# A two-layer hybrid encoder on one core: the mixers' modulation pieces stand earlier in the weight order

## The chip, the cores and the metric

One core of a Trainium2 chip runs the whole program. The metric is device time in microseconds (us) of one execution, as the median of several runs. Engines are named as the profile names them: PE is TensorE's matmul, PEld its weight load, DVE is VectorE, ACT is ScalarE, POOL is GpSimd, SP is SyncE, which here only issues DMAs.

## The reference

The kernel computes two layers on one sequence of 256 tokens with 1024 channels, all in float32. Cut to what matters here:

```
mod = silu(c) @ ada_w + ada_b                       # c is one row; ada_w is 1024 x 6144 per layer
sh_m, sc_m, gt_m, sh_f, sc_f, gt_f = split(mod, 6)
h = rms_norm(x, g_pre_mix) * (1 + sc_m) + sh_m
rq, rk, rv, rg, lx, ly, fq, fk, fv, ff, gates = split(h @ w_in)
y_ret = silu(rg) * head_norm(retention(rope(rq), rope(rk), rv))
y_lru = gelu(ly) * rg_lru(causal_conv(lx))
y_fox = forgetting_attention(fq, fk, fv, log_sigmoid(ff + b_f))
merged = g0 * (y_ret @ ret_w_o) + g1 * (y_lru @ lru_w_o) + g2 * (y_fox @ fox_w_o)     # g = sigmoid(gates)
x = x + gt_m * rms_norm(merged @ w_out, g_post_mix)
h = rms_norm(x, g_pre_mlp) * (1 + sc_f) + sh_f
x = x + gt_f * rms_norm(square(relu(h @ w1)) @ w2, g_post_mlp)
```

The first half of a layer is called the mixer, the second the MLP. `mod` is a product of one row with a large matrix: its weights must be read (24 MB per layer), but there is little to compute. `gt_m`, `sc_f` and `sh_f` are first used at the end of the mixer.

## The kernel before

**Weights come in pieces.** Every weight matrix is cut into pieces of 1 MB. A piece is loaded as two halves of 512 KB (128 partitions x 1024 float32, tile `wraw`) by the DMA queue of SP. There are five `wraw` buffers (`NRAW`). All pieces of the program stand in one list, `ORDER`, and both the loads and the preparation of the pieces follow it.

**What happens to a matmul piece** (an entry `gemm`). Each half is split in a high and a low part, because three matmuls of rounded operands replace one in float32: ACT casts it to the high part (L241) and DVE subtracts that from the original (L242); both write one of four `wpair` buffers (`NHL`). The subtraction is the last reader of the `wraw` buffer, so it frees it for the next load. PE then runs the three products of each pair (L364, L365, L366), 48 matmuls of 256 columns for a piece. A result lies in PSUM (`ps`, two buffers for most pieces, four of another pool for `lx`, `ly` and the attention) until DVE or ACT has taken it out.

**What happens to a modulation piece** (an entry `ada`). PE has no part in it. DVE multiplies each half with the row of `silu(c)` and sums along it in one instruction (L296), which also frees the buffer; a small addition of the bias follows (L292). A part such as `gt_m` is four pieces. ACT does nothing for it.

**What sets the order.** Each engine runs its own instructions in the order that the program's scheduler has written down; an instruction that waits holds up all behind it on its engine. Pieces are asked for one or two ahead of their matmuls: `prefetch` walks `ORDER`, splits what is a matmul piece and sums what is a modulation piece as it comes to it. `weight_order` builds the list: within a mixer, `spread` puts the modulation pieces evenly between the matmul pieces from position `n - MIXR[l][0]` to position `n - MIXR[l][1]`, with n = 53 matmul pieces in the mixer of layer 0 and 61 in that of layer 1. The MLPs have their own modulation pieces (`MLPR`).

**The mixer's order of matmul pieces** after the first ones is `rg0..3 g12 w_r0..3 g13 ly0..3 fq0 w_l0..3 fv0..3 fq1..3 fk0..3 g20..3 w_f0..3 w_o0..3` (with `lru` before `rg`). During `rg`, `g12` and `w_r` DVE also runs the gates of the recurrent branch (L710 to L715) and its scan (L723 to L728); during `ly` the gelu (L903 to L906, and L678 for the low part of its result, `yll`). `w_l0` needs the results of all four `ly`. From `fk1` on the heads of the forgetting attention run beside the weights (L950 to L991).

Layer 0 has 12 modulation pieces in its mixer (`gt_m`, `sc_f`, `sh_f`, 24 halves), layer 1 has 8 (`sc_f`, `sh_f`, 16 halves). Before, they stand from behind `fv1` to ahead of `g23` in layer 0, and from behind `fv3` to ahead of `g23` in layer 1.

Of the kernel before, what the change touches and what calls it, by code (L numbers as in the profile page):

```python
# [69 lines left out]
def mix_order(l):  # L70
    first = 'g0 g0 g0 g0 lx lx g1 lx g1 lx lru' if l == 0 else \
            'rv rv rv rv rq rk g0 rq rk g0 lx g0 lx g0 lx g1 lx lru g1'
    rest = 'rg rg rg rg g1 w_r w_r w_r w_r g1 ly ly ly ly fq w_l w_l w_l w_l fv fv fv fv fq fq fq fk fk fk fk ' \
           'g2 g2 g2 g2 w_f w_f w_f w_f w_o w_o w_o w_o'
    order = first.split() + rest.split()
    return [(n, order[:i].count(n)) for i, n in enumerate(order)]
# [10 lines left out]
    return name in ('rv', 'w_o', 'w2') or (name == 'w1' and cix < 4)  # L87


MIXR = ((22, 8), (20, 8))  # L90
MLPR = ((5, 28), (5, 15))


def weight_order():
    order = [(n, 0, k) for k in range(KD) for n in ('ada_row', 'row')]

    def spread(l, gem, ada, lo, hi):
        at = [lo + (hi - lo) * i // max(len(ada), 1) for i in range(len(ada))]
        for i, (n, c) in enumerate(gem):
            order.append(('gemm', l, n, c))  # L100
            while at and at[0] <= i:
                at.pop(0)
                order.append(ada.pop(0))
        assert not ada

    for l in range(L):
        n = len(mix_order(l))
        parts = [(l, p) for p in ('gt_m', 'sc_f', 'sh_f')][l:]
        spread(l, mix_order(l), [('ada',) + p + (c,) for p in parts for c in range(4)], *(n - i for i in MIXR[l]))
        parts = [(l, 'gt_f')] + [(i, p) for i in range(l + 1, L) for p in ('sc_m', 'sh_m', 'gt_m')]  # L110
# [1109 lines left out]
```

## Time and profile before

| what | us |
|---|---|
| median of 3 runs (1123.99 to 1126.6) | 1125.44 |
| the profiled execution's own time | 1126.98 |
| its span, first to last instruction | 1125.2 |
| PE busy in the span | 1096.8 (97%) |
| DVE busy | 870.1 (77%) |
| ACT busy | 617.5 (55%) |
| DVE's 82 sums of modulation halves (L296 on `wraw`), busy | 100.0 |
| DVE idle ahead of them, until a DMA landed | 44.6 |

Times in the profile count from the first instruction. Layer 0's mixer lies between about 60 and 375 us, layer 1's between about 580 and 925 us. A matmul row lasts 0.28 us, but the next one starts 0.11 us after it, so PE's pace is read from starts, and a busy share of 5.00 in 5 us says only that no gap was longer than a matmul. An idle time in brackets behind a row says how long the engine stood before it and who ended that.

### The profile page before, as it was taken

What the parts mean: (1) busy time and instruction counts of PE and PEld (TensorE: products, weight loads), DVE (VectorE), ACT (ScalarE), POOL (GpSimd) and SP (SyncE); (2) the same over time, 40 slices, a digit from 0 to 9 for tenths busy, and PEclk for the clock granted to TensorE, in tenths of its full rate; (3) what the DMA queues carried; (4) which work ended last, traced back from release to release, by engine and by line L of the source; (5) the groups of instructions that cost most, each with busy time, mean ns of one, the idle gap of its engine ahead of it and who ended that gap; (6) DMA issues with size and microseconds to landing.
All of it is one profiled execution on the core that took longest, in us unless ns stands there. A gap on an engine that the chain in (4) does not pass through costs nothing.

```text
span 1125.2 us, 20478 instructions
## 1 busy us (share of the span) xinstructions
PE 1096.8 (97%) x8164; PEld 1034.8 (92%) x8164; DVE 870.1 (77%) x1324; ACT 617.5 (55%) x924; POOL 43.7 (4%) x60
## 2 busy tenths in 40 slices
PE   6999999999999999999999999999999999999997
PEld 5999999998899889989879999999999997989986
DVE  6998788878887789888586768887868788866543
ACT  6676695544455645444455658755434655645441
POOL 0001000000000210000030010000000002000000
PEclk9999999999999999999999999999999999999999
DMA  9954646679876569998845465566777584875641
GB/s 359 408 179 155 197 136 216 193 248 314 282 249 220 193 214 323 332 327 295 299 140 185 151 194 162 185 207 194 235 248 265 193 290 133 283 269 197 195 159 59
DMA packets 74284, 255.43 MB, mean 227 GB/s; under 512 B 10108, under 2 KB 12492, under 8 KB 74188
## 3 DMA queue, kind: packets, MB, share of 16 engines
q1 hardware_dynamic: 74188, 254.12, 67.2%
q8 instruction: 64, 1.05, 0.4%
q14 instruction: 32, 0.26, 0.1%
HBM read 253.00 MB, written 1.09 MB: 226 GB/s over the span
## 4 chain that ended last, share of the span: by engine, by line
PE 75%; DVE 9%; DMA 8%; issue 4%; ACT 3%; POOL 1%; DVEq 0%; POOLq 0%; SPq 0%; ACTq 0%
PE ps L366 22%; PE ps L365 22%; PE ps L364 22%; DMA wraw<-in_wts_dram 7%; DVE wpair L242 3%; DVE wraw L296 1%; ACT wpair L241 1%; ACT junk L445 1%; PE rvp L364 1%; PE rvp L365 1%; PE rvp L366 1%; POOL rs_v L199 1%; PE qkp L365 1%; PE qkp L364 1%; PE qkp L366 1%
## 5 line engine op out<-in xcount | busy, mean ns | idle before, releaser
L242 DVE TENSOR_TENSOR wpair<-wraw,wpair 128x1024 fp32r<-128x1024 f32 (+1 forms) x286 | 347.3, 1220 | 74.1 <-ACT wpair L241 72.7
L241 ACT CAST wpair<-wraw 128x1024 fp32r<-128x1024 f32 (+1 forms) x286 | 298.3, 1049 | 191.4 <-PE ps L366 122.5
L364 PE MATMUL ps<-hh,wpair 128*128 128x256 f32 x1312 | 364.9, 278 | 5.3 <-DVE fvl L678 2.8
L366 PE MATMUL ps<-hh,wpair 128*128 128x256 f32 x1312 | 363.4, 277 | 0.1
L365 PE MATMUL ps<-hl,wpair 128*128 128x256 f32 x1312 | 363.1, 277 | 0.0
L364 PEld LDWEIGHTS ps<-hh,wpair 128*128 128x128 f32 x1312 | 246.8, 188 | 6.5 <-DVE fvl L678 3.2
L366 PEld LDWEIGHTS ps<-hh,wpair 128*128 128x128 f32 x1312 | 246.5, 188 | 0.4 <-DVE wpair L242 0.3
L365 PEld LDWEIGHTS ps<-hl,wpair 128*128 128x128 f32 x1312 | 246.6, 188 | 0.2
L296 DVE SCALAR_TENSOR_TENSOR wraw<-wraw,sir 128x1024 f32<-128x1024 f32 x82 | 100.0, 1222 | 44.9 <-DMA wraw<-in_wts_dram 44.6
L241 ACT CAST wown<-wraw 128x1024 fp32r<-128x1024 f32 x72 | 74.7, 1048 | 62.4 <-DMA wraw<-in_wts_dram 40.6
L242 DVE TENSOR_TENSOR wown<-wraw,wown 128x1024 fp32r<-128x1024 f32 x72 | 87.4, 1222 | 26.2 <-ACT wown L241 25.9
L364 PE MATMUL ps<-wpair,mih 128*128 128x512 f32 x144 | 56.3, 391 | 0.0
L365 PE MATMUL ps<-wpair,mih 128*128 128x512 f32 x144 | 56.1, 389 | 0.0
L366 PE MATMUL ps<-wpair,mil 128*128 128x512 f32 x144 | 56.0, 389 | 0.0
L364 PE MATMUL ps<-wpair,hh 128*128 128x256 f32 (+1 forms) x144 | 45.6, 317 | 0.0
L365 PE MATMUL ps<-wpair,hh 128*128 128x256 f32 (+1 forms) x144 | 45.4, 316 | 0.0
L366 PE MATMUL ps<-wpair,hl 128*128 128x256 f32 (+1 forms) x144 | 45.4, 315 | 0.0
L364 PE MATMUL ps<-hh,wown 128*128 128x256 f32 x160 | 44.2, 276 | 0.0
L366 PE MATMUL ps<-hh,wown 128*128 128x256 f32 x160 | 44.2, 276 | 0.0
L365 PE MATMUL ps<-hl,wown 128*128 128x256 f32 x160 | 44.2, 276 | 0.0
L364 PE MATMUL ps<-wown,mih 128*128 128x512 f32 x112 | 43.7, 390 | 0.0
L365 PE MATMUL ps<-wown,mih 128*128 128x512 f32 x112 | 43.6, 389 | 0.0
(340 smaller groups left out, 2295.1 us busy)
## 6 DMA issues: line engine op xcount, KB each, us to landing
wraw<-in_wts_dram SPq DMA_DIRECT2D x440, 512.0 KB, 4.4
wfirst<-in_wts_dram SPq DMA_DIRECT2D x28, 512.0 KB, 10.2
rows<-drow SPq DMA_DIRECT2D x10, 512.0 KB, 5.0
xs<-in_x_dram SPq DMA_DIRECT2D x2, 512.0 KB
out_dram<-xs SPq DMA_DIRECT2D x4, 256.0 KB, 2.0
csb<-in_con_dram SPq DMA_DIRECT2D x1, 768.0 KB
csb<-in_con_dram SPq DMA_DIRECT2D x1, 256.0 KB, 10.1
vsb<-in_vec_dram SPq DMA_DIRECT2D x1, 152.0 KB
```

Source lines behind the costliest of these rows:

```text
L199: pin(nc.gpsimd.tensor_scalar(v, part, rest, None, ALU.add))
L241: A.copy(hi, t)
L242: V.tensor_tensor(lo, t, hi.bitcast(F32), ALU.subtract)
L296: V.scalar_tensor_tensor(t, t, 0.5, sir, ALU.mult, ALU.mult, accum_out=m)
L364: T.matmul(ps, ah, bh, start=start, stop=False, **kw)
L365: T.matmul(ps, ah, bl, start=False, stop=False, **kw)
L366: T.matmul(ps, al, bh, start=False, stop=stop, **kw)
L445: return A.activation(j, x, AF.Square, scale=D ** -0.5, accum_out=acc)
```

## The change

The two pairs of positions are other numbers; nothing else differs.

```
-MIXR = ((22, 8), (20, 8))
+MIXR = ((36, 14), (32, 14))
```

In layer 0 the 12 modulation pieces now stand from behind `w_r1` to behind `fk0`: `gt_m` among `w_r2..ly2`, `sc_f` among `fq0..w_l3`, `sh_f` among `fv0..fk0`; one comes to every 1.83 matmul pieces, before to every 1.17. In layer 1 the 8 pieces stand from behind `ly0` to behind `fq3`: one to 2.25 pieces, before one to 1.5. The number of loads, sums and matmuls is the same, and PE's instructions stand in the same order as before. The orders of DVE, SP and ACT change.

The first place is DVE's order in layer 0, from the end of `rg3` to the first half of `w_r1`'s weights (`wpair_1992`); `wraw_2057` and `wraw_2060` are the first modulation piece, `wraw_2129` is half of the second.

```order
+L296 SCALAR_TENSOR_TENSOR wraw_2057,mcol_2056<-wraw_2057,sir_84 128x1024
 L710 SCALAR_TENSOR_TENSOR lru_u_650<-ti_1902,lru_u_650 128x512
+L296 SCALAR_TENSOR_TENSOR wraw_2060,mcol_2056<-wraw_2060,sir_84 128x1024
 L712 SCALAR_TENSOR_TENSOR lru_a_652<-lru_a_652,lru_t_651 128x512
+L292 TENSOR_TENSOR mod0_111<-mcol_2056,vsb_83 128x2
 L714 TENSOR_SCALAR lru_a_652<-lru_a_652 128x512
 L715 TENSOR_SCALAR lru_t_651<-lru_t_651 128x512
 L710 SCALAR_TENSOR_TENSOR lru_u_650<-ti_1929,lru_u_650 128x512
 L712 SCALAR_TENSOR_TENSOR lru_a_652<-lru_a_652,lru_t_651 128x512
-L714 TENSOR_SCALAR lru_a_652<-lru_a_652 128x512
+L296 SCALAR_TENSOR_TENSOR wraw_2129,mcol_2128<-wraw_2129,sir_84 128x1024
 L242 TENSOR_TENSOR wpair_1992<-wraw_1990,wpair_1992 128x4x256
```

Three sums now stand ahead of the low part of `w_r1`, and the third reads a load that takes the place of the second.

The second place is DVE's order in layer 0 where the scan ends and the first half of `ly0`'s weights is split (`wpair_2274`); `wraw_2265` and `wraw_2268` are the third modulation piece. These are rows of the changed kernel.

```order
L296 SCALAR_TENSOR_TENSOR wraw_2265,mcol_2264<-wraw_2265,sir_84 128x1024
L725 TENSOR_TENSOR lru_u_650<-lru_u_650,lru_t_651 128x512
L872 SCALAR_TENSOR_TENSOR gate_699<-gate_699,ps_2214 128x512
L728 SCALAR_TENSOR_TENSOR lru_u_650<-lru_a_652,lru_u_650 128x256
L296 SCALAR_TENSOR_TENSOR wraw_2268,mcol_2264<-wraw_2268,sir_84 128x1024
L242 TENSOR_TENSOR wpair_2274<-wraw_2272,wpair_2274 128x4x256
```

Before, the split of this half stood ahead of these three scan and merge rows, and no sum stood near it.

The third place is DVE's order in layer 1, at the start of `ly`, in the changed kernel: `wpair_8470` and `wpair_8475` are the two halves of `ly1`, `wpair_8537` is the first half of `ly2`, and `wraw_8603` and `wraw_8606` are the second modulation piece.

```order
L242 TENSOR_TENSOR wpair_8470<-wraw_8468,wpair_8470 128x4x256
L296 SCALAR_TENSOR_TENSOR wraw_8603,mcol_8602<-wraw_8603,sir_84 128x1024
L296 SCALAR_TENSOR_TENSOR wraw_8606,mcol_8602<-wraw_8606,sir_84 128x1024
L242 TENSOR_TENSOR wpair_8475<-wraw_8473,wpair_8475 128x4x256
L242 TENSOR_TENSOR wpair_8537<-wraw_8535,wpair_8537 128x4x256
L292 TENSOR_TENSOR mod1_112<-mcol_8602,vsb_83 128x2
L903 SCALAR_TENSOR_TENSOR ge_8527<-ge_8527,ps_8478 128x512
```

Before, the splits of `ly1` and `ly2` followed one another here; now two sums of a piece that is loaded behind `ly2` stand between the halves of `ly1`.

## Rows read from the trace of the kernel before

**Rows 1.** Page, part 1: busy us, share of the span, instructions.
```profile
PE 1096.8 (97%) x8164; PEld 1034.8 (92%) x8164; DVE 870.1 (77%) x1324; ACT 617.5 (55%) x924; POOL 43.7 (4%) x60
```

**Rows 2.** Busy time by stretch: length, then PE, PEld, DVE, ACT, POOL; granted clock, DMA share, GB/s.
```profile
157.00:190.00 33.00, 32.87 (x290) 32.67 (x288) 29.90 (x42) 22.51 (x30) 0.00 (x0) 1.00 0.53 174
190.00:216.00 26.00, 26.00 (x232) 26.00 (x231) 20.95 (x26) 16.96 (x23) 0.00 (x0) 1.00 0.63 202
235.00:320.00 85.00, 79.64 (x666) 78.46 (x665) 72.19 (x148) 35.05 (x54) 0.00 (x0) 0.98 0.85 292
310.00:315.00 5.00, 5.00 (x32) 5.00 (x31) 4.52 (x8) 1.07 (x3) 0.00 (x0) 0.66 0.83 253
728.00:744.00 16.00, 16.00 (x144) 16.00 (x142) 14.70 (x20) 7.73 (x8) 0.00 (x0) 1.00 0.65 210
744.00:771.00 27.00, 27.00 (x241) 27.00 (x240) 22.54 (x27) 17.36 (x24) 0.00 (x0) 1.00 0.65 208
798.00:870.00 72.00, 69.21 (x591) 68.19 (x590) 56.14 (x116) 31.09 (x49) 0.00 (x0) 1.00 0.78 260
```

**Rows 3.** Timeline of PE: start, duration, instruction, idle before and who ended it.
```profile
183.99 0.28 PE L364 MATMUL ps<-hh,wpair 128*128 128x256 f32 x1
...
260.81 0.28 PE L366 MATMUL ps<-wpair,hl 128*128 128x256 f32 x1
262.37 0.38 PE L364 MATMUL ps<-hh,wpair 128*128 128x256 f32 x1 [1.28 <-DVE fvl L678]
...
269.64 0.39 PE L364 MATMUL ps<-hh,wpair 128*128 128x256 f32 x1 [1.49 <-DVE fvl L678]
...
292.95 0.39 PE L365 MATMUL fs<-fkl,fqh 128*128 128x256 f32 x1 [0.28 <-DVE fkl L678]
...
307.23 0.33 PE L974 MATMUL ft<-csb,sm 128*128 128x128 f32 x1 [1.21 <-DVE sm L968]
...
308.89 0.33 PE L974 MATMUL ft<-csb,sm 128*128 128x128 f32 x1 [1.11 <-DVE sm L968]
...
833.41 0.39 PE L364 MATMUL ps<-hh,wpair 128*128 128x256 f32 x1 [1.97 <-DVE fql L914]
...
853.00 0.38 PE L364 MATMUL ps<-hh,wpair 128*128 128x256 f32 x1 [0.55 <-DVE fkl L678]
...
867.18 0.39 PE L364 MATMUL fo<-pth,fvh 128*128 128x256 f32 x1 [0.27 <-DVE ptl L678]
```

**Rows 4.** Timeline of DVE in layer 1, columns as above.
```profile
829.24 1.23 DVE L296 SCALAR_TENSOR_TENSOR wraw<-wraw,sir 128x1024 f32<-128x1024 f32 x1 [3.81 <-DMA wraw<-in_wts_dram]
...
831.53 1.22 DVE L296 SCALAR_TENSOR_TENSOR wraw<-wraw,sir 128x1024 f32<-128x1024 f32 x1
...
832.67 0.68 DVE L914 SCALAR_TENSOR_TENSOR fql<-ps,fqh 128x512 fp32r<-128x512 f32 x1
```

**Rows 5.** Line L296 from 228 to 330 us: DVE idle before it, us and times.
```profile
  DMA wraw<-in_wts_dram: 12.2, 12
```

**Rows 6.** Chain that ended last: start, duration, what.
```profile
230.29 4.12 DMA wraw<-in_wts_dram
...
822.51 6.70 DMA wraw<-in_wts_dram
```

**Rows 7.** Timeline of ACT in layer 0.
```profile
176.03 1.05 ACT L241 CAST wpair<-wraw 128x1024 fp32r<-128x1024 f32 x1 [1.62 <-PE ps L366]
178.75 1.06 ACT L241 CAST wpair<-wraw 128x1024 fp32r<-128x1024 f32 x1 [1.67 <-PE ps L366]
```

**Rows 8.** Timeline of DVE in the `ly` stretches of both layers.
```profile
195.70 0.69 DVE L903 SCALAR_TENSOR_TENSOR ge<-ge,ps 128x512 f32<-128x512 f32 x1 [1.04 <-ACT ge L902]
...
216.62 0.68 DVE L678 TENSOR_TENSOR yll<-ge,ylh 128x512 fp32r<-128x512 f32 x1
...
748.91 0.69 DVE L903 SCALAR_TENSOR_TENSOR ge<-ge,ps 128x512 f32<-128x512 f32 x1 [1.04 <-ACT ge L902]
...
769.83 0.68 DVE L678 TENSOR_TENSOR yll<-ge,ylh 128x512 fp32r<-128x512 f32 x1
```

## The prediction

> **What bounds the kernel now.** I began with the busy times of the page: PE is busy for 97% of the span [rows 1], so only two things can change the time, a stretch in which PE stands or runs slowly, and a stretch in which it begins to. Next I read the busy times by stretch [rows 2]. Where no modulation piece is in the way PE runs at one matmul per 0.113 us (232 in 26 us from 190 to 216). From 235 to 320, layer 0's stretch of modulation pieces, it is busy for 79.64 of 85 us, and from 798 to 870 in layer 1 for 69.21 of 72; the DMA engines are 0.85 and 0.78 busy there against 0.53 to 0.65 in the stretches ahead. Then I listed PE's waits in these two stretches [rows 3]. All are for DVE: for the low part of a value or key (fvl, fql, fkl), which frees a PSUM buffer or feeds the scores, or for the softmax (sm). Last I asked why DVE was late. Its timeline shows it [rows 4]: a sum of a modulation half (L296) stood 3.81 us until its load landed, another followed, and the fql that PE was waiting for stood behind both. In layer 0 the sums waited 12 times for 12.2 us in total [rows 5]. The load at the end of that chain is one issued as soon as a buffer came free, and it took 4.12 us in one place and 6.70 in another [rows 6]. So the bound in these stretches is the round of the five raw buffers, seen by PE through DVE's strict order.
>
> **The change part by part: what goes away.** A wait costs PE its bracket and about 0.28 us around it: between the rows at 260.81 and 262.37 lie 1.56 us of which 0.11 is the normal step, the following step is 0.11 too long, and the bracket says 1.28. By this the waits of rows 3 cost 1.56, 1.77, 0.56, 1.4 and 1.3 us in layer 0 (6.6), and 2.25, 0.83 and 0.55 in layer 1 (3.6). There is a second loss behind the two softmax waits: from 310 to 315 the granted clock is 0.66, and PE has 32 matmuls where 46 are usual (5 / 0.113, and the two that reach over the edges) [rows 2]; 0.66 is a mean over time at 1.2 and at 2.4 GHz, ahead of it PE had stood twice with only a few short transposes between. 14 x 0.113 = 1.6 us. Together 11.8 us.
>
> I count all of this as removed but 0.7 us. The softmax and the keys from fk1 on have no sum beside them any more in either layer, so the waits from 292 on and at 853 and 867 lose their cause, and with them the slow clock. In fv, fq and fk0 sums remain (8 halves in each layer), but thinner: one modulation piece to 1.83 and 2.25 matmul pieces instead of 1.17 and 1.5. A matmul piece takes PE 5.44 us: ACT's casts, each released by PE at the end of half a piece, are 2.72 us apart [rows 7]. So five buffers have to go round in 5 x 5.44 / (2 + 2/1.17) = 7.3 us before in layer 0, and 8.8 us after; in layer 1 in 8.2 before and 9.4 after. The load takes 4.1 to 6.7 of it, cast and subtraction 1.05 and 1.14. The stretch that had 8.2 us (layer 1 before) lost 3.6 us over 72; with 8.8 and 9.4, and half as many sums in the stretch, I leave 0.7 for both.
>
> **What is added.** The sums go to stretches in which DVE is already full. From 157 to 190 (recurrent gates, scan, merges) it is busy for 29.90 of 33 us, from 190 to 216 (gelu) for 20.95 of 26 [rows 2]. A sum takes 1.14 us of DVE (831.53 to 832.67 in rows 4). The time that decides is when the last yll of the gelu is ready, since w_l0 needs it. PE begins g13 at 183.99 [rows 3]; six pieces later, at 183.99 + 6 x 5.44 = 216.6, it begins w_l0, and it reads the last quarter of yll after 36 of 48 matmuls, at 220.7. The last yll began at 216.62 and was there at about 217.3 [rows 8]. Slack: 3.4 us.
>
> Layer 0: twelve sums (gt_m and the first two pieces of sc_f) now stand ahead of that yll on DVE: 12 x 1.14 = 13.7 us. If they fill all idle time of both stretches, 3.1 + 5.05 = 8.15 us, 5.6 us of lateness remain, less the slack 2.1 us. If they fill none of the idle time of the first stretch and half of the second, it is 13.7 - 2.5 - 3.4 = 7.8 us. Idle time there is mostly DVE waiting for ACT, which waits for PE, and much of that can be filled; but some sums will themselves wait for a load, as the one at the first place of the order does: it reads a load that can be issued only when the second sum is done, so DVE stands about 1 us before it, with the low part of w_r1 behind it. I take 4.3 us, with PE standing at three places: a little at w_r1 and w_r3, about 2 us at ly0, whose first half is split behind two sums and three scan and merge rows, and the rest at w_l0.
>
> Layer 1: the scan is done when the sums begin. ly0 ends 0.83 us ahead of its L903 in layer 0 (194.87, by the pieces' starts, and 195.70), so at 748.1 here, w_l0 begins at 769.8, and the slack to the last yll (769.83 + 0.6) is again 3.5 us. Seven sums stand ahead of it: 8.0 us, against 1.3 us idle from 728 to 744 and 4.5 us from 744 to 771. With all of it filled, the cost is nothing. But at the third place of the order the sums of a piece that is loaded behind ly2 stand between the two halves of ly1. Their loads are issued only when ly0's second and ly1's first half are split; at 4.1 to 5 us a load, DVE stands some 3 to 4 us there, and ly1's second half, ly2 and ly0's gelu are queued behind it. 8.0 + 4.0 - 5.8 - 3.5 = 2.7; I take 2.6, bounds 0 and 4.
>
> The Trainium skill ("DMA: Bandwidth & Descriptors", section "Anatomy of one DMA") fits a transfer as about 2.0 us plus its bytes at 436 GB/s, for another issuing path, which for 512 KB is an estimate of 3.2 us; by that page DVE's stand in layer 1 would be about 1 us shorter and that term 1.6. The rows here say 4.12 to 6.70, and they decide.
>
> PE, ACT and SP get nothing new to do; the modulation parts are needed only at w_f, so having them earlier gains nothing.
>
> **The sum.** -11.8 + 0.7 + 4.3 + 2.6 = -4.2 us: 1126.98 to 1122.8 for the profiled execution (its span 1125.2 to 1121.0). That execution was 1.5 us above the median of the runs, so I forecast 1125.44 - 4.2 = 1121.2.
>
> **The rivals.** (a) DVE's idle time takes nearly all the sums in: costs 2.1 and 0, residue 0.2; -9.5 us, 1115.9. For it: PE was not kept waiting anywhere from 190 to 216 or 728 to 771. Against it: the order puts sums that wait for loads ahead of splits that PE needs next.
>
> (b) The waits move with the pieces or stay: fv and fq still have 16 sums in front of the results that free PSUM, and a third of the old losses returns (3.5 us instead of 0.7). -11.8 + 3.5 + 6.9 = -1.4 us, 1124.0, no change that can be told. For it: the losses at 262, 269 and 833 were all in fv and fq, where sums remain. Against it: rows 2 show DVE with 13 us idle of 85 there even before. The Trainium skill ("Perfetto Trace Analysis", section "Optimization Strategy") reads the same gap repeated over a stretch as a possible lack of buffers for the next tile. The number of buffers is not changed here, so by that page the gaps would come back wherever the pieces stand; the trace agrees as far as each such wait begins with a load that waited for a buffer.
>
> (c) The other side: the five raw buffers become the pace of the stretch in which DVE is full. From 157 to 216 there are 59 / 2.72 = 21.7 matmul halves and 12 sums, 6.7 rounds of five buffers, 8.75 us each; from 728 to 771 there are 15.8 + 7, 4.6 rounds of 9.4 us. A round is load, cast, subtraction and the time in DVE's queue. From a round of about 10.7 us the change loses: 59 us become 72, less 3.4 of slack, and 43 become 49, less 3.5. At 11.2 us it costs 13 + 5, so -11.8 + 0.7 + 18 = +6.9 us, 1132.3. It takes loads of 5 to 6 us and a backlog of 3 us on DVE at once. For it: DVE is 91% busy from 157 to 190, and a late subtraction delays the load that the next sum waits for. Against it: the DMA engines are only 0.53 and 0.63 busy there, so loads should be near 4 us.
>
> **How the numbers follow.** Forecast 0.44 (its own range 1118 to 1123), (a) 0.16, (b) 0.22, (c) 0.18. 0.2% is 2.25 us, about what a measurement of this kernel can tell from no change: faster 0.60, same 0.22, slower 0.18. The range for 8 in 10 runs from near (a)'s 1115.9 to the first part of (c): 1115.5 to 1128.5.
>
> **What would show it.** In the profile after: PE's waits for fvl, fql, fkl and sm gone or under 0.3 us each, and no granted clock under 0.9 around the first softmax; DVE at or near 100% from 157 to 195, new PE waits of 1 to 3 us around ly0 and w_l0 in layer 0, ended by DVE (wpair or yll); an idle time of DVE of 2 to 4 us before an L296 at the start of ly in layer 1. I am wrong if waits for fvl or fql over 1 us remain (b), if PE's new waits add up to more than 12 us (c), or if they are under 3 us (a).

## The result: slower by 0.7%

The changed kernel takes 1132.27 us (median of 3 runs, 1131.11 to 1133.04) against 1125.44 us before: ratio 1.0068, 95% interval 1.0051 to 1.0084. The forecast was 1121.2, its range 1115.5 to 1128.5; it was wrong, in its direction too. The profiled execution has a span of 1131.2 us against 1125.2.

Of the profile after, these two lines are PE's busy time, which stands beside [rows 1], and the shares of the chain of work that ended last.

```profile
PE 1098.6 (97%) x8164; PEld 1035.6 (92%) x8164; DVE 869.9 (77%) x1324; ACT 616.8 (55%) x924; POOL 43.0 (4%) x60
...
PE 65%; DVE 16%; DMA 8%; issue 4%; ACT 4%; POOL 1%; SPq 0%; DVEq 0%; POOLq 0%; ACTq 0%
```

The busy times are those of before. The chain is not: before, PE had 75% of it and DVE 9%, so DVE has 7 points more.

The busy times by stretch show where; the columns are those of [rows 2].

```profile
157.00:190.00 33.00, 32.16 (x278) 31.57 (x278) 31.12 (x50) 19.98 (x28) 0.00 (x0) 1.00 0.65 215
190.00:216.00 26.00, 24.41 (x215) 24.21 (x214) 24.77 (x37) 14.79 (x19) 0.00 (x0) 1.00 0.86 297
235.00:320.00 85.00, 83.72 (x718) 82.90 (x717) 66.57 (x128) 40.71 (x63) 0.00 (x0) 1.00 0.73 248
744.00:771.00 27.00, 25.41 (x218) 24.84 (x217) 21.25 (x30) 13.34 (x18) 0.00 (x0) 1.00 0.76 249
771.00:798.00 27.00, 25.74 (x222) 25.29 (x221) 22.95 (x34) 12.83 (x15) 0.00 (x0) 1.00 0.79 258
815.00:820.00 5.00, 2.70 (x14) 2.70 (x15) 4.59 (x7) 1.21 (x2) 0.00 (x0) 0.77 0.63 206
798.00:870.00 72.00, 67.89 (x572) 67.43 (x571) 51.48 (x96) 31.80 (x48) 0.00 (x0) 0.98 0.68 228
```

Read it against [rows 2]: layer 0's old bad stretch, 235 to 320, is nearly clean (83.72 of 85 us busy, before 79.64). The stretches from 157 to 216 and from 744 to 798 now have gaps. And 798 to 870, from which 3.6 us were to go, has become worse: 67.89 busy of 72, before 69.21.

PE's waits name the places (columns as in [rows 3]).

```profile
192.35 0.38 PE L366 MATMUL ps<-hh,wpair 128*128 128x256 f32 x1 [1.59 <-DVE wpair L242]
...
224.97 0.38 PE L365 MATMUL ps<-yll,wpair 128*128 128x256 f32 x1 [0.77 <-DVE yll L678]
...
260.51 0.39 PE L364 MATMUL ps<-wpair,hh 128*128 128x256 f32 x1 [0.62 <-DVE fvl L678]
...
752.39 0.38 PE L366 MATMUL ps<-hh,wpair 128*128 128x256 f32 x1 [1.51 <-DVE wpair L242]
...
776.84 0.39 PE L364 MATMUL ps<-ylh,wpair 128*128 128x256 f32 x1 [0.56 <-ACT ylh L907]
777.93 0.39 PE L365 MATMUL ps<-yll,wpair 128*128 128x256 f32 x1 [0.70 <-DVE yll L678]
...
806.13 0.39 PE L365 MATMUL ps<-wpair,hh 128*128 128x256 f32 x1 [1.46 <-DVE wpair L242]
...
817.30 0.38 PE L364 MATMUL ps<-wpair,hh 128*128 128x256 f32 x1 [2.65 <-DVE fvl L678]
```

Laid over the starts of the same matmuls before, PE is 0.3 us early at 157, 4.3 us late behind the wait at `w_l0` (224.97) and 5.15 late after the wait at 260.51 in layer 0. It is 1.5 us early at 313, because the waits of [rows 3] from 262 to 309 and the slow clock are gone. Behind layer 0 another 1.3 us goes at 567, at the transposes between the layers. PE enters layer 1 0.3 us early. Layer 1 then costs 6.4 net: 4.35 us up to and with `w_l0` (4.04 late), another 6.4 from there to 821 us (10.45 late), and 4.4 regained by 874, since the old waits at 833, 853 and 867 are gone. The 6.4 are the waits at 806 and 817 and about 1.6 for 16 matmuls behind the second, whose starts lie 0.21 us apart in place of 0.11: the granted clock from 815 to 820 is 0.77, a mean over time at 1.2 and at 2.4 GHz, and ahead of it PE had stood for 2.65 us.

Why PE waits at 817 is seen on DVE (columns as in [rows 4]).

```profile
748.75 1.23 DVE L296 SCALAR_TENSOR_TENSOR wraw<-wraw,sir 128x1024 f32<-128x1024 f32 x1 [4.09 <-DMA wraw<-in_wts_dram]
...
790.13 1.22 DVE L296 SCALAR_TENSOR_TENSOR wraw<-wraw,sir 128x1024 f32<-128x1024 f32 x1 [3.78 <-DMA wraw<-in_wts_dram]
...
803.10 1.22 DVE L296 SCALAR_TENSOR_TENSOR wraw<-wraw,sir 128x1024 f32<-128x1024 f32 x1 [3.46 <-DMA wraw<-in_wts_dram]
...
815.41 1.22 DVE L296 SCALAR_TENSOR_TENSOR wraw<-wraw,sir 128x1024 f32<-128x1024 f32 x1 [1.05 <-DMA wraw<-in_wts_dram]
...
827.64 1.23 DVE L296 SCALAR_TENSOR_TENSOR wraw<-wraw,sir 128x1024 f32<-128x1024 f32 x1 [3.37 <-DMA wraw<-in_wts_dram]
```

DVE stands at the first sum of every modulation piece. From 790 on, four weight halves lie between one such sum and the next, 4 x 2.72 = 10.88 us of PE's work. The sums are 12.97, 12.31 and 12.23 us apart: over these cycles PE goes at that pace. Its links are in the chain that ended last (start, duration, what).

```profile
783.40 1.23 DVE wpair L242
784.64 5.39 DMA wraw<-in_wts_dram
...
790.13 0.13 DVE wraw L296
...
796.66 1.26 DVE wpair L242
797.94 5.07 DMA wraw<-in_wts_dram
...
803.10 0.13 DVE wraw L296
...
809.36 1.22 DVE wpair L242
810.61 4.78 DMA wraw<-in_wts_dram
...
816.64 0.61 DVE fvl L678
817.25 0.04 issue
817.30 0.38 PE ps L364
```

A split (L242) frees a buffer; the load into it takes 5.39 us; DVE stands for it, and then has 6.53 us in its order (two sums, two splits, merges of gates) before the split that frees the buffer for the next such load. One link is 13.26 us, the next 12.70, where PE needs 10.88: 2.4 and 1.8 us lost. Here the stand is a part of a loop through buffer, load and DVE's queue.

### The profile page after: what moved, and what is told of

Read it like the earlier page. It is cut to its first block, busy times and chain, and to the rows that moved or that the text cites. A ratio compares the mean times of both kernels' runs of the same rounds, so it can differ in the third digit from the quotient of the medians.

```text
span 1131.2 us, 20476 instructions
## 1 busy us (share of the span) xinstructions
PE 1098.6 (97%) x8164; PEld 1035.6 (92%) x8164; DVE 869.9 (77%) x1324; ACT 616.8 (55%) x924; POOL 43.0 (4%) x60
## 4 chain that ended last, share of the span: by engine, by line
PE 65%; DVE 16%; DMA 8%; issue 4%; ACT 4%; POOL 1%; SPq 0%; DVEq 0%; POOLq 0%; ACTq 0%
PE ps L366 19%; PE ps L364 19%; PE ps L365 19%; DVE wpair L242 6%; DMA wraw<-in_wts_dram 6%; DVE wraw L296 2%; ACT wpair L241 1%; DVE lru_u L728 1%; PE rvp L364 1%; POOL rs_v L199 1%; PE rvp L365 1%; PE rvp L366 1%; PE qkp L364 1%; PE qkp L365 1%; PE qkp L366 1%
## 5 line engine op out<-in xcount | busy, mean ns | idle before, releaser
L242 DVE TENSOR_TENSOR wpair<-wraw,wpair 128x1024 fp32r<-128x1024 f32 (+1 forms) x286 | 347.0, 1220 | 76.6 <-ACT wpair L241 74.9
L296 DVE SCALAR_TENSOR_TENSOR wraw<-wraw,sir 128x1024 f32<-128x1024 f32 x82 | 99.9, 1220 | 47.7 <-DMA wraw<-in_wts_dram 47.4
L242 DVE TENSOR_TENSOR wown<-wraw,wown 128x1024 fp32r<-128x1024 f32 x72 | 87.3, 1221 | 25.7 <-ACT wown L241 25.3
## 6 DMA issues: line engine op xcount, KB each, us to landing
wfirst<-in_wts_dram SPq DMA_DIRECT2D x28, 512.0 KB, 10.2
```

The costliest lines, as they stand in the source:

```text
L242: V.tensor_tensor(lo, t, hi.bitcast(F32), ALU.subtract)
L296: V.scalar_tensor_tensor(t, t, 0.5, sir, ALU.mult, ALU.mult, accum_out=m)
```

## Experiments

Three theories. **Order** (theory 1): the stands in front of what PE needs next cost the time. **Work** (rival 2): the sums' own 1.14 us each, in full stretches. **Round** (theory 3, formed after the first eight runs): neither alone, but the loop just shown, of load and work together, through five buffers.

| run | median, us | ratio to before, 95% |
|---|---|---|
| e1_l0 | 1122.77 | 0.9987 (0.9978 to 0.9997) |
| e2_l1 | 1134.12 | 1.0083 (1.0067 to 1.0099) |
| e3_short | 1118.48 | 0.9952 (0.9935 to 0.9969) |
| e4_nowait | 1126.88 | 1.0019 (1.0004 to 1.0034) |
| e4_pinned | 1119.88 | 0.9966 (0.9953 to 0.9980) |
| d1_after | 1128.64 | 1.0040 (1.0025 to 1.0054) |
| d3_l1 | 1122.67 | 0.9987 (0.9973 to 1.0002) |
| p5_before | 1145.22 | 1.0201 (1.0184 to 1.0217) |
| p5_after | 1151.33 | 1.0236 (1.0218 to 1.0254) |
| n6_before | 1147.41 | 1.0197 (1.0179 to 1.0215) |
| n6_after | 1147.65 | 1.0201 (1.0184 to 1.0218) |
| w8 | 1121.72 | 0.9981 (0.9966 to 0.9995) |
| b1 | 1120.84 | 0.9965 (0.9952 to 0.9979) |
| b2 | 1125.27 | 1.0015 (1.0001 to 1.0029) |
| b3 | 1122.58 | 0.9988 (0.9975 to 1.0001) |
| pad96 | 1147.72 | 1.0207 (1.0192 to 1.0222) |

In these the kernel before had medians of 1123.8 to 1124.45 us. A kernel's executions differ by some us (`b2`: 1121.85 to 1130.74), and each trace shows one of them; where that one lies far from its median, the text says so.

**One layer at a time.**

```
e1_l0:  MIXR = ((36, 14), (20, 8))      e2_l1:  MIXR = ((22, 8), (32, 14))
```

> Only layer 0's mixer gets the new places (36 and 14 pieces from the end), layer 1 keeps the old ones (20 and 8). If the time of the change is lost where DVE stands in front of late loads in layer 1 (theory 1), this kernel gives layer 0's balance alone: in the traces PE lost 5.15 us up to the first value piece of layer 0 and had gained 1.5 us net by 313 us, so about 1124 us, 0.9987 of before. If the twelve sums ahead of the gelu's last yll simply add their DVE work to the time and the old waits do not pay it back (rival 2), it is 2 us or more over before, 1127 to 1130.

> Only layer 1's mixer gets the new places (32 and 14), layer 0 keeps the old ones (22 and 8). Theory 1: all of the loss is in layer 1, so 1125.4 + 6 to 7.5 = 1131.5 to 1133 us, slower than the changed kernel or equal to it, with PE waits of over 1 us for fvl or wpair between ly1 and fv1. Rival 2 (the loss is shared by the layers, by DVE work): 1127 to 1129.

Measured: -1.5 us and +9.3 us against before; together 7.9, and the whole change is 7.7 (0.68% of 1125). Layer 0's part of the forecast had the right sign; layer 1 alone is more than the whole loss. That e2_l1 is slower than the changed kernel was foreseen; its size is 1 us over the range given.

**The work taken out, loads and waits kept.** In the mixers' modulation pieces the sums go over 64 of the 1024 columns.

```
-            ada_sum(raw_half(j), m[:, j:j + 1])
+            if mix:
+                t = raw_half(j).rearrange("p k c -> p (k c)")[:, :64]
+                V.scalar_tensor_tensor(t, t, 0.5, sir[:, :64], ALU.mult, ALU.mult, accum_out=m[:, j:j + 1])
...
```

> The changed kernel with every load and every wait of the mixers' modulation sums left, but each of these sums cut from 1024 columns to 64 (the other columns of these sums are left out), so that 40 sums cost DVE about 0.1 us in place of 1.14. Theory 1 (DVE stands in order for loads that are issued late): the stands stay, above all in layer 1, and only the lateness of layer 0 from DVE's work goes: 1127 to 1130 us. Rival 2 (the 1.14 us of DVE's own work is what is late): the old waits and the new are both gone, 1113 to 1117 us.

Measured 1118.48: far below what theory 1 said, and 1.5 over rival 2's range. (The profiled execution took 1122.53.) Yet DVE's first sums stand as long as in the changed kernel (DVE's timeline, then the busy times of two stretches).

```profile
785.02 0.23 DVE L304 SCALAR_TENSOR_TENSOR wraw<-wraw,sir 128x64 f32<-128x64 f32 x1 [3.55 <-DMA wraw<-in_wts_dram]
...
796.28 0.23 DVE L304 SCALAR_TENSOR_TENSOR wraw<-wraw,sir 128x64 f32<-128x64 f32 x1 [3.52 <-DMA wraw<-in_wts_dram]
...
817.64 0.23 DVE L304 SCALAR_TENSOR_TENSOR wraw<-wraw,sir 128x64 f32<-128x64 f32 x1 [3.79 <-DMA wraw<-in_wts_dram]
```

```profile
216.00:235.00 19.00, 16.92 (x141) 16.12 (x140) 14.09 (x30) 9.78 (x12) 0.00 (x0) 1.00 0.80 262
...
798.00:870.00 72.00, 72.00 (x629) 71.95 (x628) 47.77 (x105) 35.55 (x57) 0.00 (x0) 1.00 0.67 226
```

From 798 to 870 the stands are there and PE has no gap. The cycle is now 11.26 us from 785.02 to 796.28, and 21.36 for the next two, PE's own pace: two sums less (2 us) in the link. So a stand is not the loss by itself: theory 1 as I stated it falls. Two places still lose time without the work, by the matmuls' starts: `w_l0` of layer 1 (1.9 us, against 4.35 for `ly` and `w_l0` in the changed kernel), and `w_l0` of layer 0 (3.1 us; its gaps are in the first row), while `w_r` and `ly` ahead of that lose nothing.

**The loads taken out, the work kept.** The mixers' modulation weights are left out; their sums run over a row that is always there.

```
-            ada_sum(raw_half(j), m[:, j:j + 1])
+            if part in ('sc_f', 'sh_f') or (l, part) == (0, 'gt_m'):
+                V.scalar_tensor_tensor(sir, sir, 1.0, sir, ALU.mult, ALU.max, accum_out=m[:, j:j + 1])
...
```

> The changed kernel with the mixers' modulation pieces not loaded (their weights are left out of the computation): the sums run at full width in the same order on a row that is always there, so DVE has the same work but waits for no load and takes no raw buffer. Theory 1: the stands go, what stays is layer 0's 4 us of DVE work ahead of the gelu and perhaps 1 to 2 us in layer 1, against 11.8 us of old waits gone: 1117 to 1121 us. Rival 2 (DVE's work): within 2 us of the changed kernel, 1130 to 1132 us.

Measured 1126.88, between the two, but it can't be read: without a load to wait for, the scheduler put many sums elsewhere. From 400 to 728 us DVE has 400 instructions in place of 366, and PE loses 5 us more there than in the changed kernel. With each sum held behind the weight split ahead of it (`with tc.issue_after(last[0].ins):`) they stay near their places, though not all in them: in layer 1 the first sum of some pieces now stands behind a split that it stood ahead of.

> As the run without loads (the mixers' modulation pieces are not loaded, their sums run at full width on a resident row), but each sum is held behind the last weight split ahead of it, so that the sums stay at the changed kernel's places on DVE. Work without waits. If DVE's work of 1.14 us a sum is by itself what makes PE late (rival 2), layer 1 still loses its 6 to 7 us between ly and fv: 1128 to 1132 us. If it takes work and late loads together (theory 3: five buffers whose round holds a load, a cast, a split and DVE's queue), layer 1 loses nothing and layer 0 only the 3 to 5 us of twelve sums ahead of the last yll: 1116 to 1120 us.

```profile
190.00:216.00 26.00, 23.84 (x196) 23.65 (x196) 24.84 (x38) 13.76 (x18) 0.00 (x0) 0.93 0.53 169
...
728.00:798.00 70.00, 70.00 (x617) 70.00 (x616) 65.42 (x94) 36.43 (x45) 0.00 (x0) 1.00 0.63 199
798.00:870.00 72.00, 72.00 (x629) 71.95 (x628) 51.11 (x105) 35.05 (x56) 0.00 (x0) 1.00 0.52 170
```

Measured 1119.88, in theory 3's range. DVE has more to do from 728 to 798 than in the changed kernel (65.42 us against 60.20), and layer 1 loses nothing. The work alone is not the loss either: rival 2 falls for layer 1, as far as these places of the sums tell; `d3_l1` below says the same with every load kept. In layer 0 PE still waits 2.8 us for weights at `w_r3` and `ly0` (157 to 216), without a load of a sum to wait for. Behind the second of these waits, 2.15 us long, it runs at 1.2 GHz for a while (granted clock from 190 to 216: 0.93). By the matmuls' starts that makes 5.5 us, and nothing at `w_l0`. So in layer 0 neither kernel is free of the loss: without the work it is 3.1 us, without the loads 5.5, with both 4.6.

**The stands taken out, everything else kept.** A sum half is issued behind the split of the next weight half that follows it:

```
-        V.tensor_tensor(lo, t, hi.bitcast(F32), ALU.subtract)
+        i = V.tensor_tensor(lo, t, hi.bitcast(F32), ALU.subtract)
+        if owed:
+            with tc.issue_after(i.ins):
+                owed.pop(0)()
...
+            owed.extend((lambda: half(0), lambda: half(1)))
```

> The changed kernel with the mixers' sums held back on DVE: each half's sum stands behind the subtraction of a half of the next weight piece instead of ahead of it; loads, work and buffers are the same. Theory 1: DVE stands less in front of the splits that PE needs (a load has 2.7 to 5.4 us more), so 1122 to 1128 us; if the buffers that are held longer pass the delay to the loads of the next weight pieces, the gain is given back and it stays at 1130 to 1135 us, and the round of five buffers as a whole, not the order on DVE, is the pace. Rival 2: unchanged, 1131 to 1133 us.

> The changed kernel with the sums of layer 1 alone held back behind the split of the next half piece; layer 0 as in the changed kernel. In the run with both layers held back layer 1 lost 2 us of PE time and layer 0 about 8. If the layers stand apart, layer 0's balance of -1.5 us stays and layer 1's comes to -1 from +6: about 1123 us. If holding back makes the following weight loads late in layer 1 as it did in layer 0: 1128 us or more.

Both layers: 1128.64, between the two ranges given. Layer 0 alone has 7.9 us of gaps from 157 to 320 (4.6 in the changed kernel), most of them for splits of weights that come late; that the buffers, held longer, make them late was not followed up. Layer 1 alone (`d3_l1`): 1122.67, as expected, 9 us below the changed kernel with the same loads, sums and buffers. Its sums from 728 to 798 (line by line: busy us, mean ns, idle before) and its stretches:

```profile
L301 DVE SCALAR_TENSOR_TENSOR wraw<-wraw,sir 128x1024 f32<-128x1024 f32 x10 | 12.2, 1220 | 0.0
```

```profile
728.00:798.00 70.00, 69.15 (x605) 68.76 (x604) 62.79 (x85) 35.45 (x42) 0.00 (x0) 1.00 0.79 257
798.00:870.00 72.00, 72.00 (x629) 71.95 (x628) 53.11 (x109) 35.47 (x58) 0.00 (x0) 1.00 0.69 237
```

The changed kernel's ten sums there stood 9.7 us; now none, and PE's gaps from 728 to 870 go from 7.0 to 0.85 us.

**A sixth buffer.** Its room comes from smaller pads behind the tiles, which cost 2% on their own, and from a few small tiles, so there are four kernels with the same small pads and tiles.

```
-NRAW = 5                    # p5: stays 5;  n6: 6
-SLOT_PAD = 128
+SLOT_PAD = 64
...
```

> The changed kernel with six raw buffers in place of five; the room comes from smaller pads behind the weight tiles and single small tiles in the forget gate's logarithm. Theory 1 (a load that waits for one of five buffers, with DVE standing in order before its sum): each load is issued about one half piece (2.7 us) earlier, stands of 3 to 4 us in layer 1 shrink to about 1 us or nothing, and most of layer 1's 6 us and some of layer 0's go: 1121 to 1126 us. If DVE's own work is the cause (rival 2), the sixth buffer changes nothing: 1130 to 1133 us.

> The control of the six buffers: the changed kernel with the same smaller pads and single small tiles, but five raw buffers. Both theories expect the changed kernel's time, 1132 us; a difference is the price of the pads and has to be taken off the run with six.

> The kernel before with six raw buffers and the smaller pads. Theory 1: its own waits of 11.8 us in the two stretches are also made by the round of five buffers, so most of them go, 1116 to 1121 us; then the places of the pieces matter little once there are six. Rival 2: 1124 to 1126 us.

> The kernel before with five raw buffers and the smaller pads, the partner of the two runs with six buffers, 1147.7 and 1147.4 us, and of the changed kernel with five, 1151.3. If the sixth buffer also frees the kernel before from waits of its own (theory 3), this is 2 to 5 us over the run with six, 1149 to 1153 us. If the round of buffers matters only where the change put the pieces: 1147 us, or less by up to 3.

The expectations for `n6_after`, `p5_after` and `n6_before` failed by about 20 us, the price of the pads; that for `p5_before`, made when this price was known, came out by its second branch. The comparison among the four stands: with five buffers the change costs 1151.33 - 1145.22 = +6.1 us, with six 1147.65 - 1147.41 = +0.2. `p5_before` ran later than the other three; by the ratios, each to the kernel before as run beside it, the change costs 0.35% (3.9 us) with five and 0.04% with six. In the stretch from 798 to 870 (five buffers, then six, both changed):

```profile
798.00:870.00 72.00, 67.52 (x550) 66.66 (x549) 49.85 (x88) 28.77 (x38) 0.00 (x0) 0.98 0.69 236
```

```profile
798.00:870.00 72.00, 69.82 (x588) 69.36 (x587) 53.06 (x96) 32.43 (x46) 0.00 (x0) 1.00 0.72 236
```

Most of the loss belongs to the round of five buffers; with six PE still has gaps of 2.2 us here, in place of 4.5. The expectation that the kernel before would also gain was wrong: by the medians it is 2.2 us slower with six, by the ratios the same (1.0197 and 1.0201). The Trainium skill ("Perfetto Trace Analysis", section "Optimization Strategy") takes a gap repeated over a stretch as a possible lack of buffers. For the changed kernel these runs agree (3.7 us less with six); for the kernel before they don't.

**Thinner pieces.**

```
w8:  MIXR = ((36, 8), (32, 8))       b1:  MIXR = ((36, 14), (32, 8))
b2:  MIXR = ((28, 8), (32, 8))       b3:  MIXR = ((32, 8), (32, 8))
```

> The changed kernel with the pieces spread over more weight pieces: from 36 to 8 pieces before the end in layer 0 and from 32 to 8 in layer 1, one to every 2.33 and 3 weight pieces, so that some sums stand beside the attention's keys again. Theory 3 (the round of five buffers is the pace): there is 9.5 and 10.2 us for a round in place of 8.8 and 9.4, fewer sums stand ahead of each result, and most of layer 1's loss and half of layer 0's go: 1117 to 1122 us. If sums beside the keys and the softmax cost what they cost before, whatever the density: 1125 to 1128 us.

> Layer 0's pieces as in the changed kernel (36 to 14), layer 1's thinner (32 to 8, one to every 3 weight pieces). If the density in layer 1 alone made the loss (theory 3), layer 0's balance of -1.5 us and layer 1's of -2.6 add up: 1121 us. If layer 1 was lost by where its pieces begin (32, among the last gates, the same as in the changed kernel): 1128 us or more.

> Layer 1 as in b1 (32 to 8); layer 0 from 28 to 8, behind the gelu's matmuls, one piece to every 1.67 weight pieces. DVE has no sums from the gates to ly, where it is booked out; the round of five buffers has 8.3 us in place of 7.3 in the kernel before. Theory 3: layer 0 loses 2 to 3 us in place of the 5.5 before and nothing ahead of w_l: 1119 to 1121 us. If the density of 1.67 is as bad there as 1.17 was (the waits stay beside the values and queries): 1122 to 1124 us.

> Layer 1 as in b1; layer 0 also from 32 to 8, one piece to every 2 weight pieces, beginning at the last output gate piece, behind the recurrence's gates. Theory 3: fewer sums in the full stretch than from 36 and more time for a round (8.8 us) than in b2: layer 0 loses 1 to 3 us, 1118 to 1121 us. If any sum ahead of the last yll is paid in full at w_l: 1123 us or more.

w8 and b1 came as expected. b1 is 0.35% (3.9 us) faster than before, 11 us below the changed kernel, and the fastest kernel here that does all the work, though not clear of w8. (Its profiled execution, 1117.6 us, is the fastest of its six.) In its layer 1 three weight pieces (16.32 us) lie between two modulation pieces; DVE stands about as long, and PE has no gap:

```profile
779.81 1.23 DVE L296 SCALAR_TENSOR_TENSOR wraw<-wraw,sir 128x1024 f32<-128x1024 f32 x1 [3.15 <-DMA wraw<-in_wts_dram]
...
795.89 1.23 DVE L296 SCALAR_TENSOR_TENSOR wraw<-wraw,sir 128x1024 f32<-128x1024 f32 x1 [2.27 <-DMA wraw<-in_wts_dram]
...
812.68 1.23 DVE L296 SCALAR_TENSOR_TENSOR wraw<-wraw,sir 128x1024 f32<-128x1024 f32 x1 [3.77 <-DMA wraw<-in_wts_dram]
```

```profile
728.00:798.00 70.00, 70.00 (x615) 70.00 (x615) 61.02 (x85) 35.64 (x43) 0.00 (x0) 1.00 0.76 252
798.00:870.00 72.00, 72.00 (x629) 71.95 (x628) 54.77 (x118) 36.88 (x64) 0.00 (x0) 1.00 0.70 234
```

b2 failed: 1125.27 where 1119 to 1121 was expected (its other branch, 1122 to 1124, missed too), although its density (one to 1.67) is lower than before (1.17). The profiled execution is its slowest, 1130.74 us, so the trace shows a bad case. Its 17 sums from 235 to 320 stood 23.2 us (24 sums for 12.2 before). The worst place, in the chain:

```profile
290.62 1.15 DVE wpair L242
291.78 6.71 DMA wraw<-in_wts_dram
298.58 0.13 DVE wraw L296
298.72 1.02 issue
299.82 0.61 DVE fkl L678
300.48 0.39 PE fs L365
```

A load issued by the split just ahead, 6.71 us, a key's low part behind the sum: PE stood 3.83 us. So density is not all of it; by this place, what DVE's order puts between the freeing split, the sum and the result that PE needs counts too, but no run tried that by itself in layer 0. b3, at one to 2, lost 5.0 us in the same stretch and missed its range by 1.6.

**The pads alone** (`SLOT_PAD = 96`, nothing else).

> The kernel before with pads of 96 in place of 128 floats behind each weight tile and nothing else. The runs with small pads and five or six buffers were 2% slower with PE busy all the time: 163 matmuls in 19 us in place of 170. If the pads do that, by where the weights lie in SBUF: 1135 to 1147 us. If it was one of the other moves there (the tiles ahead of them taken out, the low parts of the first value piece moved): 1124 to 1126 us.

Measured 1147.72, +2.07%, 0.7 us over the range given for the pads: they do it.

## Why the prediction was wrong

The sizes here are differences between the starts of the same matmuls.

**The old waits (-11.8)** measured -12.8. In layer 0 the waits for `fkl` and `sm` are gone and the granted clock from 235 to 320 is 1.00 (before 0.98): PE's matmuls from 240 to 320 take 79.95 us before and 71.50 where PE has no gap (`e4_pinned`), so 8.5 us were to be had there. In layer 1 the three waits went, 4.4 us, but others took their place earlier. That the old waits came from the round of five buffers, as the prediction has it, no run bears out: with six buffers and small pads the kernel before gained nothing.

**What is left of them (+0.7): the step that failed.** "With 8.8 and 9.4, and half as many sums in the stretch, I leave 0.7 for both." It measured 6.4 us in layer 1, where 1.6 of it is the slow clock, and 2.6 in layer 0 (the same matmuls from 240 to 320 take 74.08 us after). Two things were wrong in it. The 9.4 us were worked out from the mean of 2.25 weight pieces; six of the seven distances, and all from 790 on, are exactly two, which allows 5 x 10.88 / 6 = 9.1 us for five buffers. And the round was taken as load, cast and subtraction, 6.3 to 9 us, with DVE's order left out: six halves took 12.2 to 13.0 us, so five take 10.2 to 10.8, of which the load is 4.8 to 5.4. By the runs, taking out the load (e4_pinned, with the sums slightly moved), the sums' work (e3_short) or their place in the order (d3_l1) each removes these 6.4 us, and so does one weight piece more in the cycle (b1).

**DVE's lateness in layer 0 (+4.3)** measured 4.6, at the places named: 0.4 at `w_r1`, 0.9 at `w_r3`, 1.9 at `ly0`, 1.5 at `w_l0`. The size and the places came out; how much of it is the sums' work and how much their loads stays open, since without the work 3.1 us are lost and without the loads 5.5.

**Layer 1's `ly` (+2.6)** measured 4.35. The stand that I foresaw is there (4.09 us, forecast 3 to 4), with `ly1`'s second half behind it. The sum counted only what arrives late at `w_l0`; 1.8 us went at `ly1` itself, where PE waited 1.51 us for that half's split (752.39). Without the sums' work 1.9 us of the 4.35 stay, with the sums held back 1.4, without their loads nothing.

Together: -12.8 + 9.0 + 4.6 + 4.35 and the 1.3 at 567 are +6.4 us; up to 157 us 0.3 was gained, and the spans differ by 6.0.

**The rivals.** (c) named the right loop, DVE's queue as a part of the round, and its sign came (new losses of 18 us, over 12), but it put the loop at 157 to 216 and 728 to 771. Its time, 1132.3, is right by chance: those stretches cost 4.6 and 4.35, where (c) has 13 and 5; the loop closed behind them, at the values of layer 1, where I had called it safe. The Trainium skill ("DMA: Bandwidth & Descriptors", section "Anatomy of one DMA") has a fit, for another issuing path, by which such a load is an estimate of 3.2 us; the loads of the chains shown here took 4.78 to 6.71.

Open: why layer 0, with two weight pieces to a modulation piece from 235 on, goes round in 10.6 to 11.7 us and loses less there, and the 1.3 us at 567, which are not in all of these kernels.

## What to carry to other kernels

When work is thinned out over a buffer ring, follow one buffer through a whole round as the chain shows it, with all that the freeing engine does in order between two frees, and compare it with what the bound engine needs at the local spacing, not the mean. Here long waits in front of an instruction cost nothing where they did not close such a loop (`e3_short`, `b1`), and shortening any one link (the load, the work, the order) took the loop's loss away. Where a change acts in two places, time each by itself: here one was worth -1.5 us and the other +9.

## What the runs showed of the hardware

Not expected before the sixth buffer was tried: the pads change PE's pace. They stand behind the tiles of split weights and behind those of activations. With 96 in place of 128 floats, and nothing else changed, PE runs without a gap from 216 to 235 us and does 164 matmuls (first row) where the kernel before does 170 (second):

```profile
216.00:235.00 19.00, 19.00 (x164) 19.00 (x163) 14.30 (x16) 8.80 (x10) 0.00 (x0) 1.00 0.63 196
```

```profile
216.00:235.00 19.00, 19.00 (x170) 19.00 (x170) 13.16 (x15) 8.13 (x9) 0.00 (x0) 1.00 0.71 203
```

From 190 to 216 it is 222 in place of 232 [rows 2], 0.117 us each in place of 0.112, at a granted clock of 1.00. Which of the tiles' addresses does it was not tried.
